# Hybrid decoder step: rooms for the first FFN weights, two tile scalings and the last output-projection units

## Chip, cores and metric

One Trainium2 chip, one core. The metric is the device time of one execution in microseconds. The kernel before runs in 2260.09 us (median of three runs, 2257.26 to 2260.82); the execution that the profiler recorded took 2260.48 us.

## What is computed

One layer of a hybrid decoder, for a prompt of 1024 tokens and a sample of 8 sequences with 8 tokens each. The part that matters here, from the reference:

```python
h = h + jnp.concatenate([o_gla, o_mla], axis=-1) @ lw['w_o']
y, conv_new = conv_ffn(rmsnorm(h, lw['g_ffn']), conv_prev, lw)
h = h + y
...
def conv_ffn(n, prev, lw):
    a = n @ lw['ffn_w_gate']
    c = n @ lw['ffn_w_up']
    ...
    y = (jax.nn.silu(conv) * c) @ lw['ffn_w_down']
```

`o_mla` of the sample comes from attention over a paged cache of 8192 past tokens for each of the 8 sequences; that is 64 blocks of 128 x 8 cached rows. `w_o` is 1024 x 1024, `ffn_w_gate` and `ffn_w_up` are 1024 x 2816.

## The kernel before, in words

All matrices are float32, held as a high and a low part (`split`, lines 115 to 117: ScalarE casts the high part, VectorE or GpSimd subtracts to get the low part), and a product is three matmuls (`mm3`, lines 139 to 141).

The work before the FFN is two interleaved programs. The *dense* one projects the prompt, runs its linear attention and its latent attention. The *cache stream* (`cache_stream`, L678) takes the 64 blocks of the sample's cache, n = 0 to 63. Block n passes through stages that overlap with those of its neighbours: `main` multiplies the pages with the absorbed weights (line 139 to 141, tile `ks`), ScalarE squares (L560), VectorE sums each two pages (L565, four such *slots* in a block); `stage_b` turns the sums into scaled scores (ACT L586 to L588, DVE L589 and L590, POOL L592 and L594, DVE L598 for the maxima, POOL L599), and splits the pages for the second product (ACT L603, POOL L604); `stage_c1` transposes the maxima on TensorE (tile `mt`, L616 and L625), subtracts and exponentiates (DVE L626, ACT L628 and L629, POOL L630); `stage_pv` multiplies with the pages (`cpv`, L645); `stage_c2` finishes a sequence after its last block (L667 to L676).

When the dense program has ended, 47 of the 64 blocks are done, and the output projection's *units* (`wo_units`, L1536) become the filler of the rest: a unit is one row tile t of 128 tokens, one half f of the 1024 columns, and a pair of the eight 128-row slices of `w_o`: six matmuls of 512 columns (L1432, L1435, L1436) and one addition into the residual on VectorE (L1439). There are four pairs, so 4 x 16 units; the generator's first step only loads. `place` (L574) is called at each slot and issues one unit from the seventh slot on, except at every eighth, until the counter is 49, that is until the first three pairs are through. The last pair's 16 units run through the tiles in the order 6, 7, 0, 3, 1, 4, 2, 5, both halves of a tile together. With a tile's second half its residual is complete and `normed` (L1587) follows: ScalarE squares and sums both halves (L1465), GpSimd makes the scale (L1466, L1467), ScalarE's queue stores the tile to DRAM (L1591), and `xnorm` (L1469) multiplies by the scale and the gain. `xnorm` has two forms, chosen by a bit mask `VIAP` over the tiles: one VectorE instruction (L1474), or a scaling on ScalarE (L1476) and a multiplication by the gain on GpSimd (L1477).

In the stream's *drain*, the last three steps with hardly any blocks left, the units are issued by hand. With "63rd" and "64th" for the blocks n = 62 and n = 63, the counts before are: 1 in `stage_c1` of the 63rd (and whatever is missing to 49), 3 in its `stage_pv`, 2 and 1 in `stage_c1` of the 64th, 5 in its `stage_pv`, 4 in its `stage_c2`.

Then come the FFN's operands. `turned_rest` transposes tiles 6 and 7 (L132, tile `xr`), `turned_pair` (L1657) transposes the pairs (0, 3), (1, 4), (2, 5) (L1663) and forms the sums of a Strassen-like scheme with seven products on blocks of 384 tokens: ScalarE's copies and casts (L1665, L116), VectorE's and GpSimd's sums and low parts (L1666 to L1672, L117). `down_sample` adds the sample's part (`ps_ds`, L1445, L1448), several rooms of SBUF are closed, `last_sums` splits the last two operands `t3` and `t4` (six casts on ScalarE, three subtractions each on GpSimd and VectorE), `normed(NT)` normalises the sample's 64 rows `hs`, and `ff_weights(0)` (L1699) loads and splits the first chunk of 128 FFN columns: four DMAs of 256 KB on SyncE's queue (L1705, tile `st`), eight operands in splits (`g0`, `g1`, `s2`, `s1`, `s4`, `s3`, `u1`, `u0`; casts of tile `wh`, low parts of tile `wl`), and between them four sums on GpSimd (L1712, L1713 for `s1` and `s2`; L1716, L1718 for `s4` and `s3`). `ff_chunk` (L1753) runs the seven products of tile `ps_gu` in the order g0, g1, s2, s1, s4, s3, u1, and the rest of the rows. There are 22 chunks.

The order of each engine's queue isn't the order of the text: the kernel is built with `schedule_with_timeline_sim=True`, and the framework sets each queue's order at build time by a model of the timeline, with the text's order as the priority. `behind()` (L570) and `keep_in_program_order` bind some TensorE work to its place.

Of the kernel before, what the change touches and what calls it, by code (L numbers as in the profile page):

```python
# [29 lines left out]
PLAN = ([0], [], [1, 2, 3])  # L30
VIAP = 20
GS0 = 1
# [13 lines left out]
def step_kernel(ctx: ExitStack, tc: tile.TileContext, A):  # L46
# [152 lines left out]
    z = {}  # L199
# [374 lines left out]
    def place():  # L574

        z["slot"] += 1
        if z["slot"] > 6 and z["slot"] % 8 and z["units"] < 49:
            fill(1)
# [27 lines left out]
    def stage_c1(o):  # L606
# [4 lines left out]
        drain = o.n - NB * 8 + 3  # L611
        if drain == 1:
            fill(49 - z["units"])
        elif drain == 2:
            fill(2)
        pe.transpose(mt[:, 0:P], o.ml.rearrange("p a c -> p (a c)"), ident)  # L616
# [21 lines left out]
    def stage_pv(o):  # L638
        nt, phl = o.nt, o.phl
        drain = o.n - NB * 8 + 3  # L640
        if drain > 0:
            fill(1 + 2 * drain)
        o.pv = pv = pm([P, 512], "cpv")
        for i in range(nt):
            pe.matmul(pv[:, 0:258], phl[:, i, :], o.ch[:, i, :], start=i == 0, stop=i == nt - 1)  # L645
        if (o.b, o.bi) == (NB - 1, 7):
            acc = z["late"][:, 0:258]
        else:
            acc = cp.tile([P, 258], F32, tag="pvs", name="pvs", bufs=2)
        if o.t is None:  # L650
            act.copy(acc, pv[:, 0:258])
        else:
            dve.scalar_tensor_tensor(acc, sums.pop(o.b), o.t, pv[:, 0:258], ALU.mult, ALU.add)
        sums[o.b] = acc

    def stage_c2(o):
# [15 lines left out]
        if b == NB - 1:  # L672
            fill(4)
        pt = pm([P, 512], "pt_ol")
# [919 lines left out]
    def fill(n):  # L1594
        for _ in range(n):
            z["units"] += next(z["fill"], done) is None
# [102 lines left out]
    def ff_weights(f):  # L1699
# [14 lines left out]
        w["s2"] = block(s2, dve)  # L1714
        w["s1"] = block(s1, dve)
        pool.tensor_tensor(g1, g1, s2, ALU.subtract)  # L1716
        w["s4"] = block(g1, dve)
# [35 lines left out]
    def ff_chunk(f):  # L1753
# [33 lines left out]
        if f + 1 < NF:  # L1787
            ff_weights(f + 1)
        conv(0, NP)
# [55 lines left out]
    rx2 = opened("xh2", side="right")  # L1845
    xb.update({nm: [z["xh2"].tile([P, 4, NP], F32R, name=f"x{nm}{s}") for s in "hl"] for nm in ("t4", "t3")})
    for t in range(3):
        last_sums(t)
    normed(NT)
    room["hp"].close()  # L1850
    fw, fv = opened("fw", side="right"), opened("fv", side="right")
    ff_weights(0)
    rt = opened("tp")
# [271 lines left out]
```

## Time and profile before

| | us |
|---|---|
| median of three runs | 2260.09 |
| profiled execution | 2260.48 |
| its span, first to last instruction | 2258.8 |
| around the span | 1.7 |
| TensorE busy | 2169.4 (96%) |
| VectorE busy | 1674.5 (74%) |
| ScalarE busy | 1338.8 (59%) |
| GpSimd busy | 1242.1 (55%) |

Times of rows are microseconds from the span's start. In a row of the timeline the columns are start, length, engine, line, operation, tile written and tiles read, shape, count; the bracket at the end is the engine's idle time just before the instruction and what ended it. Matmuls overlap: what a matmul costs TensorE is the distance from its start to the next one's. PEclk is the granted clock of TensorE as a share of its upper level.

### The profile page before, as it was taken

What the parts mean: (1) busy time and instruction counts of PE and PEld (TensorE: products, weight loads), DVE (VectorE), ACT (ScalarE), POOL (GpSimd) and SP (SyncE); (2) the same over time, 40 slices, a digit from 0 to 9 for tenths busy, and PEclk for the clock granted to TensorE, in tenths of its full rate; (3) what the DMA queues carried; (4) which work ended last, traced back from release to release, by engine and by line L of the source; (5) the groups of instructions that cost most, each with busy time, mean ns of one, the idle gap of its engine ahead of it and who ended that gap; (6) DMA issues with size and microseconds to landing.
All of it is one profiled execution on the core that took longest, in us unless ns stands there. A gap on an engine that the chain in (4) does not pass through costs nothing.

```text
span 2258.8 us, 38778 instructions
## 1 busy us (share of the span) xinstructions
PE 2169.4 (96%) x13591; PEld 1962.1 (87%) x13591; DVE 1674.5 (74%) x2608; ACT 1338.8 (59%) x3711; POOL 1242.1 (55%) x1332
## 2 busy tenths in 40 slices
PE   7999989999999999998999988999999999999999
PEld 6889978878888888887888877999999997888899
DVE  5775776467788888886878878888888876777642
ACT  5676766777778898886777765333333334222531
POOL 5675677567777777675454468656565640010200
PEclk9899999999999999999999988999999999999999
DMA  5343334413342222213322122332323224333131
GB/s 183 113 135 100 91 120 147 139 50 88 83 122 59 60 79 67 59 41 129 98 66 77 62 98 76 98 104 84 103 84 105 83 81 133 113 122 117 52 116 40
DMA packets 193461, 213.43 MB, mean 94 GB/s; under 512 B 41198, under 2 KB 145107, under 8 KB 193267
## 3 DMA queue, kind: packets, MB, share of 16 engines
q1 hardware_dynamic: 179603, 164.02, 23.5%
q0 software_dynamic: 12432, 42.48, 6.1%
q10 hardware_dynamic: 1232, 4.46, 0.5%
q8 instruction: 109, 1.79, 0.3%
q14 instruction: 85, 0.70, 0.1%
HBM read 168.34 MB, written 42.52 MB: 93 GB/s over the span
## 4 chain that ended last, share of the span: by engine, by line
PE 81%; DVE 7%; ACT 5%; DMA 3%; POOL 2%; issue 2%; SPq 0%; ACTq 0%; POOLq 0%; DVEq 0%
PE ps_gu L140 7%; PE ps_gu L141 7%; PE ps_gu L139 7%; PE ks L139 5%; PE ks L141 4%; PE ks L140 4%; PE ps_dn L139 4%; PE ps_dn L140 4%; PE ps_dn L141 4%; PE cpv L645 2%; PE ctp L522 2%; PE ps_lt L278 2%; PE ps_pj L139 2%; PE ps_pj L140 1%; PE ps_pj L141 1%
## 5 line engine op out<-in xcount | busy, mean ns | idle before, releaser
L560 ACT ACTIVATE csq<-ks 128x256 f32<-128x256 f32 x1040 | 392.5, 400 | 87.9 <-PE ks L141 79.2
L565 DVE TENSOR_REDUCE css<-csq 128x16 f32<-128x1024 f32 (+1 forms) x264 | 315.8, 1197 | 64.6 <-ACT csq L560 61.8
L116 ACT CAST wh<-st 128x512 fp32r<-128x512 f32 x176 | 108.4, 619 | 186.1 <-PE ps_gu L140 161.4
L139 PE MATMUL ks<-mv0h,cTh 128*128 128x320 f32 (+1 forms) x520 | 171.7, 332 | 6.6 <-ACT csq L560 2.9
L139 PE MATMUL ks<-mv1h,cTh 128*128 128x320 f32 (+1 forms) x520 | 170.6, 330 | 7.6 <-ACT sn L562 3.6
L604 POOL TENSOR_TENSOR chl<-craw,chl 128x1024 fp32r<-128x1024 f32 x64 | 141.3, 2208 | 57.6 <-ACT chl L603 57.0
L140 PE MATMUL ks<-mv1l,cTh 128*128 128x320 f32 (+1 forms) x520 | 154.0, 298 | 0.0
L140 PE MATMUL ks<-mv0l,cTh 128*128 128x320 f32 (+1 forms) x520 | 152.9, 296 | 0.0
L141 PE MATMUL ks<-mv0h,cTl 128*128 128x320 f32 (+1 forms) x520 | 148.5, 298 | 0.9 <-DVE cTl L117 0.8
L141 PE MATMUL ks<-mv1h,cTl 128*128 128x320 f32 (+1 forms) x520 | 148.8, 300 | 0.0
L630 POOL TENSOR_TENSOR phl<-sn,phl 128x512 fp32r<-128x512 f32 (+1 forms) x64 | 84.9, 1327 | 108.2 <-ACT phl L629 107.8
L1928 DVE TENSOR_TENSOR h<-h,ps_dn 128x512 f32<-128x512 f32 x160 | 107.7, 685 | 49.0 <-PE ps_dn L141 43.2
L117 DVE TENSOR_TENSOR wl<-st,wh 128x512 fp32r<-128x512 f32 x132 | 119.0, 903 | 29.6 <-ACT wh L116 29.6
L139 PE MATMUL ps_dn<-w,s 128*128 128x512 f32 x352 | 137.0, 393 | 2.3 <-ACT w L116 2.3
L140 PE MATMUL ps_dn<-w,s 128*128 128x512 f32 x352 | 137.6, 391 | 0.0
L141 PE MATMUL ps_dn<-w,s 128*128 128x512 f32 x352 | 136.9, 390 | 0.0
L1939 POOL TENSOR_TENSOR h<-h,raw 128x512 f32<-128x512 f32 x16 | 20.7, 1294 | 195.5 <-DMA raw<-dh 133.5
L117 POOL TENSOR_TENSOR wl<-st,wh 128x512 fp32r<-128x512 f32 x44 | 69.5, 1581 | 104.9 <-ACT wh L116 104.9
L117 DVE TENSOR_TENSOR cTl<-ctp,cTh 128x512 fp32r<-128x512 f32 (+1 forms) x136 | 90.1, 662 | 39.1 <-ACT cTh L116 38.1
L139 PEld LDWEIGHTS ks<-mv0h,cTh 128*128 128x128 f32 x520 | 98.9, 190 | 20.6 <-ACT sn L562 7.2
L139 PEld LDWEIGHTS ks<-mv1h,cTh 128*128 128x128 f32 x520 | 99.7, 192 | 19.4 <-ACT sn L562 7.0
L562 ACT COPY sn<-ks 128x64 f32<-128x64 f32 x520 | 116.4, 224 | 0.0
(662 smaller groups left out, 7974.3 us busy)
## 6 DMA issues: line engine op xcount, KB each, us to landing
stage<-w_in SPq DMA_DIRECT2D x48, 256.0 KB
st<-ffn_w_gate SPq DMA_DIRECT2D x44, 256.0 KB
st<-ffn_w_up SPq DMA_DIRECT2D x44, 256.0 KB
wr<-ffn_w_down SPq DMA_DIRECT2D x44, 256.0 KB
raw<-ds SPq DMA_DIRECT2D x44, 256.0 KB
raw<-ffn_w_down SPq DMA_DIRECT2D x44, 256.0 KB
ds<-cv SPq DMA_DIRECT2D x21, 512.0 KB
oraw<-doT SPq DMA_DIRECT2D x16, 256.0 KB
```

The lines of the kernel that those rows point to most:

```text
L116: act.copy(hi, src)
L117: (lo_eng or dve).tensor_tensor(lo, src, hi.bitcast(F32), ALU.subtract)
L139: pe.matmul(ps, ah, bh, start=first, stop=False)
L140: pe.matmul(ps, ah, bl, start=False, stop=False)
L141: return pe.matmul(ps, al, bh, start=False, stop=last)
L278: pe.matmul(ps, x, w, start=first, stop=last)
L560: act.activation(sq[:, f * 256:f * 256 + 256], ks[:, 0:256], AF.Square)
L562: act.copy(o.sn[:, g0 + i, :], ks[:, 256:320])
L565: dve.tensor_reduce(o.ss[:, g0 + i + 1 - n:g0 + i + 1, :].rearrange("p i h -> p (i h)"), sq2[:, :n].rearrange("p i (h n) -> p (i h) n", n= ...
L604: pool.tensor_tensor(ch[:, c0:c1, 128:256], src, ch[:, c0:c1, 0:128].bitcast(F32), ALU.subtract)
L630: pool.tensor_tensor(phl[:, :nt, 64:128], sb, phl[:, :nt, 0:64].bitcast(F32), ALU.subtract)
L1928: dve.tensor_tensor(h[:, t, cs], h[:, t, cs], ps, ALU.add)
```

## The change

Three things are changed. The mask `VIAP` becomes 192, tiles 6 and 7, where it was 20, tiles 2 and 4. `place` waits four slots after the counter has reached 49 and then issues one unit of the last pair at each slot, up to the counter 55, and the counts in the drain are changed: 1 and 1 in `stage_c1` of the 64th block, 3 in each `stage_pv`, all that is left in `stage_c2`. The room `fw` (the first four weight operands and the stages of the weights) is opened before `last_sums`, and `ff_weights` becomes a generator in two parts: the first part (loads, splits of `g0`, `g1`, `s2`, `s1` and the two sums that make `s1` and `s2`) stands before `last_sums` for the first chunk, the second part where it was.

```diff
-VIAP = 20
+VIAP = 192
...
         z["slot"] += 1
-        if z["slot"] > 6 and z["slot"] % 8 and z["units"] < 49:
+        if z["units"] < 49:
+            z["last"] = z["slot"] + 4
+            if z["slot"] > 6 and z["slot"] % 8:
+                fill(1)
+        elif z["slot"] > z["last"] and z["units"] < 55:
             fill(1)
...
         elif drain == 2:
-            fill(2)
+            fill(1)
...
         if drain > 0:
-            fill(1 + 2 * drain)
+            fill(3)
...
         if b == NB - 1:
-            fill(4)
+            fill(16)
...
         w["s1"] = block(s1, dve)
+        yield
         pool.tensor_tensor(g1, g1, s2, ALU.subtract)
...
-            ff_weights(f + 1)
+            for _ in ff_weights(f + 1):
+                pass
...
+    fw = opened("fw", side="right")
+    first = ff_weights(0)
+    next(first)
     for t in range(3):
         last_sums(t)
     normed(NT)
     room["hp"].close()
-    fw, fv = opened("fw", side="right"), opened("fv", side="right")
-    ff_weights(0)
+    fv = opened("fv", side="right")
+    for _ in first:
+        pass
```

## Rows read from the trace of the kernel before

**Rows 1.** The page's chain that ended last, shares of the span by engine.

```profile
PE 81%; DVE 7%; ACT 5%; DMA 3%; POOL 2%; issue 2%; SPq 0%; ACTq 0%; POOLq 0%; DVEq 0%
```

**Rows 2.** Stretches: length, busy by engine (instructions), PEclk, DMA share, GB/s.

```profile
1287.50:1312.00 24.50, 20.26 (x123) 17.50 (x121) 19.93 (x26) 17.82 (x59) 11.92 (x9) 0.93 0.13 44
1312.00:1340.30 28.30, 26.88 (x120) 21.54 (x120) 22.59 (x37) 16.86 (x42) 16.00 (x20) 0.94 0.31 121
1340.30:1362.40 22.10, 17.36 (x90) 13.03 (x89) 19.32 (x29) 16.93 (x33) 19.17 (x16) 0.77 0.29 96
1362.40:1368.30 5.90, 0.00 (x0) 0.00 (x0) 5.80 (x8) 5.65 (x13) 5.00 (x4) 0.85 0.20 44
1368.30:1390.90 22.60, 20.91 (x104) 18.89 (x104) 18.11 (x21) 11.45 (x21) 17.87 (x17) 0.89 0.27 83
1390.90:1875.00 484.10, 480.65 (x2896) 475.91 (x2896) 404.61 (x538) 182.38 (x360) 288.98 (x274) 1.00 0.29 93
```

**Rows 3.** Units' first matmuls (L1432), two stretches; L565's reductions on DVE.

```profile
1060.00:1287.50 227.50, 38.71 (x96) 18.37 (x96) 0.98 0.29 92
1287.50:1312.00 24.50, 0.79 (x2) 0.38 (x2) 0.93 0.13 44
...
1287.50:1312.00 24.50, 9.08 (x8) 0.93 0.13 44
```

**Rows 4.** Timeline of TensorE at the start of the drain.

```profile
1312.91 0.33 PE L616 MATMUL mt<-ident,ml 128*128 128x128 f32 x1 [1.87 <-POOL ml L599]
1313.75 0.43 PE L625 MATMUL mt<-ident,bm 64*128 64x64 f32 x2 [0.51 <-DVE mt L622]
...
1315.39 0.63 PE L1436 MATMUL ps_dn<-wdh,sl 128*128 128x512 f32 x1
...
1318.80 0.40 PE L1435 MATMUL ps_dn<-wdl,sh 128*128 128x512 f32 x1
1319.03 0.40 PE L1436 MATMUL ps_dn<-wdh,sl 128*128 128x512 f32 x1
```

**Rows 5.** Timeline: the scalings of tiles 6, 7 (DVE), 4 and 2 (ACT, POOL).

```profile
1321.60 1.28 DVE L1474 SCALAR_TENSOR_TENSOR h<-h,rs,gb 128x1024 f32<-128x1024 f32 x1
...
1324.62 2.34 DVE L1474 SCALAR_TENSOR_TENSOR h<-h,rs,gb 128x1024 f32<-128x1024 f32 x1
...
1340.45 1.15 ACT L1476 ACTIVATE h<-h,rs 128x1024 f32<-128x1024 f32 x1 [1.25 <-POOL rs L1467]
...
1341.68 2.35 POOL L1477 TENSOR_TENSOR h<-h,gb 128x1024 f32<-128x1024 f32 x1 [1.26 <-ACT h L1476]
...
1346.79 3.33 POOL L1477 TENSOR_TENSOR h<-h,gb 128x1024 f32<-128x1024 f32 x1 [0.22 <-ACT h L1476]
```

**Rows 6.** Timeline of ScalarE ahead of TensorE's first FFN product, and that product.

```profile
1363.23 0.63 ACT L1465 ACTIVATE junk<-hs 64x512 bf16<-64x512 f32 x1 [0.22 <-DVE hs L1456]
...
1363.86 0.60 ACT L116 CAST xt3h<-h 128x512 fp32r<-128x512 f32 x1
...
1367.66 1.12 ACT L116 CAST wh<-st 128x512 fp32r<-128x512 f32 x2
...
1368.31 0.69 PE L139 MATMUL ps_gu<-x11h,wh 128*128 128x384 f32 x1 [5.92 <-ACT wh L116]
```

**Rows 7.** Timeline of SyncE's queue: the last two loads of the first weights.

```profile
1344.74 0.92 SPq L1705 DMA_DIRECT2D st<-ffn_w_up  x2
```

**Rows 8.** Timeline of GpSimd, VectorE and TensorE in the first FFN chunk.

```profile
1364.54 4.63 POOL L117 TENSOR_TENSOR xt3l<-h,xt3h 128x512 fp32r<-128x512 f32 x3 [0.90 <-ACT xt3h L116]
...
1372.66 2.15 POOL L1713 TENSOR_TENSOR st<-st 128x512 f32<-128x512 f32 x1
...
1376.39 1.74 POOL L1718 TENSOR_TENSOR st<-st 128x512 f32<-128x512 f32 x1
...
1379.20 0.68 DVE L117 TENSOR_TENSOR wl<-st,wh 128x512 fp32r<-128x512 f32 x1
...
1380.67 0.33 PE L139 MATMUL ps_gu<-x22h,wh 128*128 128x384 f32 x1
```

## The prediction

> **What bounds the kernel now.** I began with the chain that ended last: 81% of the span lies on TensorE [rows 1]. So a change pays where TensorE stands still, or runs slowly, and nowhere else. The table of stretches says where that is [rows 2]. From 1390.9 us, soon after the start of the second FFN chunk, to 1875 us TensorE is busy 480.65 of 484.10 us: whatever comes earlier at 1390.9 ends earlier by as much. Ahead of it lie the five stretches that the change touches, 103.4 us long. TensorE is busy 85.4 us of them, so 18.0 us are idle: 4.2 at the stream's end, 1.4 in the drain, 4.7 while the operands are transposed, 5.9 in one piece before the first FFN product, 1.7 in the first chunk. Its clock is below its upper level in all five (0.77 to 0.94). The other engines tell what holds it. From 1340.3 to 1362.4 VectorE is busy 19.32 and GpSimd 19.17 of 22.10 us, so the transposes wait for the engines that empty their banks. In the 5.9 us piece nothing is missing but the first weights' high parts, which stand on ScalarE's queue behind other casts [rows 6].
>
> **Part 1, units in the stream.** How many units move follows from code and counts. By 1287.5 us the trace has 96 of the units' first matmuls, two to a unit: 48 units, so the counter is at 49, and the next ones come only with the drain, two matmuls up to 1312 us [rows 3]. Eight reductions follow 1287.5. The unit just done belongs to the first of them (with 17 blocks left there are 68 slots, and the 48th unit falls on slot 61: from slot 7 on, without 8, 16 and so on). `place` then waits for slots 62 to 65 and issues at 66, 67 and 68: three units, not the six that the limit of 55 would allow. The drain's counts then add up to 4, 7, 9, 12 and 16, against 1, 4, 7, 12 and 16 before; from the 64th block's `stage_pv` on, as many units have been issued as before. A unit is six starts of 0.23 us [rows 4], 1.4 us, so 4.2 us of matmuls go ahead of the drain. They lie where TensorE waits 1.87 us for the maxima of the 63rd block and 0.51 us for the next step [rows 4], and after that wait eight matmuls start 3.41 us apart in all (1315.39 to 1318.80) where the next distance is 0.23, eight of which are 1.84: 1.6 us lost to the lower level, 1.2 GHz, after an idle TensorE. Both gone: 2.4 + 1.6 = 4.0 us. Bounds: below, 0, if the three units only push the 64th block's `ks` matmuls, and with them its scores, by 4.2 us and the wait reopens later; above, 4.2, the whole of the moved work. I take 3.0, since both waits are for the 63rd block, which the moved units don't touch, but the 64th does start later. The additions on VectorE (three of some 0.7) fall where it is least loaded; the casts and loads of the last pair are called three slots sooner, on a SyncE queue with nothing urgent in it.
>
> **Part 2, scalings.** VectorE loses tiles 6 and 7, 1.28 + 2.34 us, and gains tiles 2 and 4 later, at 1.28 each if nothing disturbs, so its sum falls by about 1.1; ScalarE's two scalings of 1.15 and GpSimd's two products of 2.35 and 3.33 move from 1340 to 1350 us into the drain, where those engines are busy 16.9 and 16.0 of 28.3 us [rows 2, 5]. The way to tile 2's operands shortens from 1.15 + 3.33 to about 1.3 us, and GpSimd goes from the last scaling into the operands with no pause, so up to 3.2 us could come out of the transposes. Against it, VectorE, itself full there, gets 2.56 us more in that stretch, and in the drain GpSimd's scalings may stand ahead of the last block's scores. Between -3.2 and +4.7 (both products at 2.35 uncovered on the chain) I take 0, because the two late effects have about the same size and opposite sign. Clashes have a price here: the same VectorE instruction takes 1.28 us at one time and 2.34 at another, and GpSimd's 2.35 or 3.33 [rows 5], so about 1 us per meeting. The Trainium skill (SBUF — State Buffer, section "Who interferes with whom") puts it more harshly: a VectorE instruction with two SBUF inputs and a GpSimd instruction that reads SBUF exclude each other, and the later one waits for the whole of the other. By that rule the two moved products could hold VectorE for all of their length in the drain, and the sum below would end at -1.8 instead of -6.5 (the third rival). The rows show waits of 1 us, and I go by them.
>
> **Part 3, first weights.** The four loads are issued by 1345.7 us, as soon as the stages are free [rows 7], 18 us before any use; opening the room sooner moves no load. What it moves is the priority. Now the two casts of `g0` and `g1` start at 1367.66, behind six casts of `t3` and `t4` that begin at 1363.86, and TensorE starts 0.65 us after them, having waited 5.92 us [rows 6]. With the weights' casts first, they take 1363.86, and the product starts 3.8 us earlier, near 1364.5. Upper bound: the whole 5.9 us, plus 2.5 us of clock (0.89 over 22.6 us, so some 5 us at half speed), 8.4; lower: 0, see the first rival. What becomes late: `t3` and `t4` by four casts, some 2.3 us, and by GpSimd's two sums, 3.9 us by L1713 and, for the other, L1718. GpSimd's `t3` subtractions end at 1369.2 now, and the `t4` product they and VectorE feed comes after 1380.67, when the product ahead of them starts: over 10 us of cover [rows 8]. GpSimd is the next limit. It runs from 1346.79 to 1378.1 with few pauses, and the sums of `s4` and `s3` keep their place at the end of it. Now `s4`'s low part is ready at 1379.9, 0.8 us ahead of its product [rows 8]; a TensorE that is over 6 us early will wait there for one or two. I take 3.5 for the part, since the four products before that one are what it can run through first.
>
> **The sum.** 3.0 + 0 + 3.5 = 6.5 us off the profiled execution's 2260.48 (span 2258.8 and 1.7 around it), which stands 0.4 above the median: 2254.0 us, 0.27% below the median.
>
> **Rivals.** *GpSimd's queue decides.* Reordering doesn't shorten GpSimd's list, and it is busy 17.87 of 22.60 us in the first chunk and 5.00 of 5.90 before. If `s4` and `s3` come only as much earlier as GpSimd's pauses allow, 0.90 us ahead of `t3` [rows 8] and about as much again among the 2.9 us of the transposes' stretch [rows 2], TensorE starts early and waits later: 1.8 and little from part 1, about 2258. For it: the near margin at 1380.67. Against: part 1 brings GpSimd's list forward too. 15%. *The queues don't move.* Each queue's order is set by a model at build time; the weights' casts or the three units may land where they were: 2260, 7%. *VectorE is held in the drain.* If each moved product keeps VectorE's additions off for its whole 2.35 us, and these stand on the chain there, 4.7 us come back: 2260.5 - 6.5 + 4.7 = 2258.7. For it: tile 7's scaling took 1.06 us longer than tile 6's [rows 5]. Against: VectorE has 5.7 us free in the drain [rows 2]. 6%. It is what the Trainium skill's rule above would do here. *The drain stalls, and the kernel is slower.* If the scalings of tiles 6 and 7 stand on GpSimd's queue ahead of the last block's L592, L594 or L630, TensorE waits for the scores once its units are used up. Two products at 3.33 are 6.7 us, and 1.6 more at the lower clock; with part 1's gain gone and part 3's 3.5 kept that gives 2260.5 + 8.3 - 3.5 = 2265. It decides once the hold-up exceeds what the units between cover: there are five between the 64th block's maxima and its `stage_pv`, 7 us, less what the chain itself needs. For it: GpSimd's maxima already set the 1.87 us wait. Against: the queue has 12 us free in the drain. 10%.
>
> **How the numbers follow.** My forecast has the remaining 62%. The range reaches down to the sum with parts 1 and 2 near their best and part 3 between its value and its bound, 4.0 + 2.0 + 6.0 = 12 off, 2248.5, and up to no gain at all, 2260.5, which takes in the first three rivals; the slower rival and larger gains are left out. Two tenths of a per cent, 4.5 us, is about what a measurement of this kernel can tell from no change. Faster by more needs 2255.6 or less, which the forecast holds: 0.62. Within it lie the first three rivals: 0.28. Slower: 0.10.
>
> **What would show it.** Right: three units among the stream's last slots, 1305 to 1313 us, and no wait of over 1 us at the 63rd block's maxima; the first `ps_gu` matmul at 1361 us or earlier (3 from part 1, 3.8 from part 3); casts of `wh` ahead of those of `t3`; TensorE's idle time from 1287 to the second chunk down from 18 to about 12 us. Wrong: a first `ps_gu` product that comes early and a pause before that of `s4` or `s3` that takes it back; a pause at `mt` or `cpv` in the drain released by GpSimd; or a first product still behind six casts.

## The result: slower by 4 us, and the profile after

The changed kernel takes 2264.16 us (median of 22 runs, 2256.13 to 2270.58) against 2259.16 us for the kernel before, measured beside it on the same chips (22 runs): a ratio of 1.0019 [1.0011, 1.0028], so 4.3 us slower. Measured twice more, once under another name with the same order of instructions on every engine (e13 and e14 below), it gave 1.0011 [1.0002, 1.0019] and 1.0017 [1.0007, 1.0027]. The cost is thus some 2.5 to 4.3 us, where 6.5 us of gain were forecast. The profiled execution after took 2262.32 us, its span 2260.6.

The same six stretches as in [rows 2], each moved to the same event of the code, the end of the last so that its length is that of before (view: stretches; length, busy time by engine with instructions, PEclk, DMA share, GB/s):

```profile
1287.10:1311.60 24.50, 21.49 (x133) 19.24 (x132) 19.86 (x26) 18.44 (x62) 11.46 (x11) 0.93 0.19 65
1311.60:1338.30 26.70, 23.42 (x112) 18.39 (x111) 19.82 (x31) 17.41 (x42) 20.61 (x20) 1.00 0.27 101
1338.30:1363.80 25.50, 19.47 (x90) 15.07 (x88) 22.56 (x35) 15.40 (x33) 15.42 (x13) 0.67 0.29 91
1363.80:1369.80 6.00, 0.14 (x2) 0.01 (x1) 5.36 (x7) 5.60 (x13) 3.71 (x3) 0.94 0.20 44
1369.80:1392.50 22.70, 20.73 (x104) 19.43 (x105) 19.60 (x21) 11.55 (x21) 18.17 (x17) 0.87 0.27 82
1392.50:1876.60 484.10, 480.61 (x2897) 475.83 (x2896) 402.29 (x539) 182.71 (x360) 286.27 (x274) 1.00 0.29 93
```

Four lines matter. The second stretch, the drain, is 1.6 us shorter and its granted clock is up from 0.94 to 1.00. The third, the transposes, is 3.4 us longer, VectorE is busy 22.56 us of it (before 19.32) and the clock is down from 0.77 to 0.67: that takes the gain and more. The fourth, TensorE's pause before the first FFN product, is 6.00 us as against 5.90: part 3 did nothing. The last is the same to 0.3 us: from the rest rows' first product to the first down product, 484.46 us before and 484.20 after.

TensorE's timeline in the drain after, which answers to [rows 4]:

```profile
1303.83 0.40 PE L1437 MATMUL ps_dn<-wdh,sh 128*128 128x512 f32 x1
...
1306.86 0.40 PE L1437 MATMUL ps_dn<-wdh,sh 128*128 128x512 f32 x1
...
1310.80 0.39 PE L1437 MATMUL ps_dn<-wdh,sh 128*128 128x512 f32 x1
...
1313.59 0.27 PE L621 MATMUL mt<-ident,ml 128*128 128x128 f32 x1
1314.86 0.43 PE L630 MATMUL mt<-ident,bm 64*128 64x64 f32 x2 [1.00 <-DVE mt L627]
...
1321.16 1.23 PE L650 MATMUL cpv<-chl,phl 128*128 128x258 f32 x8 [0.60 <-POOL phl L635]
...
1325.45 0.33 PE L621 MATMUL mt<-ident,ml 128*128 128x128 f32 x1 [1.68 <-POOL ml L604]
```

Three units stand among the stream's last slots, and the maxima of the 63rd block (1313.59) no longer wait. But waits have reopened behind them: 1.00 us at the 63rd block's next step, 0.60 us at its `cpv` product, and at the 64th block's maxima 1.68 us, released by GpSimd's L604. Why GpSimd is late there, the timelines of ScalarE and GpSimd after tell:

```profile
1309.43 0.36 ACTq L1596 DMA_DIRECT2D dh<-h  x1
...
1314.09 1.15 ACT L1481 ACTIVATE h<-h,rs 128x1024 f32<-128x1024 f32 x1 [2.12 <-DMA dh<-h]
1315.14 0.33 ACT L591 ACTIVATE cy<-css,epst 128x64 f32<-128x64 f32 x1
...
1315.32 2.40 POOL L1482 TENSOR_TENSOR h<-h,gb 128x1024 f32<-128x1024 f32 x1 [1.45 <-ACT h L1481]
...
1318.78 1.08 POOL L597 TENSOR_TENSOR sn<-sn,cy 128x512 f32<-128x512 f32 x1
...
1322.30 2.40 POOL L1482 TENSOR_TENSOR h<-h,gb 128x1024 f32<-128x1024 f32 x1
...
1325.16 0.24 POOL L604 COPY ml<-ml 128x64 f32<-128x64 f32 x1
```

`xnorm` scales a tile in place, and `normed` stores the same tile to DRAM first. Tile 6's store is issued at 1309.43 and ScalarE, which now scales this tile, waits 2.12 us for it, until 1314.09. Behind that on its queue stands L591, the first step of the last block's scores; and the two products on GpSimd stand ahead of L597 and L604, the steps that lead to the last block's maxima. None of the prediction's sentences speaks of the store.

ScalarE ahead of the first FFN product, and that product, as in [rows 6]:

```profile
1365.41 0.60 ACT L116 CAST xt3h<-h 128x512 fp32r<-128x512 f32 x1
...
1369.14 1.12 ACT L116 CAST wh<-st 128x512 fp32r<-128x512 f32 x2
...
1369.80 0.69 PE L139 MATMUL ps_gu<-x11h,wh 128*128 128x384 f32 x1 [5.87 <-ACT wh L116]
```

The order is that of before: six casts of `t3` and `t4`, the squares, and only then the weights. Moving the code moved nothing on the queue.

To set runs side by side, the table gives times from the 62nd block's maxima (L616 before, L621 after; read from the timelines), since what lies ahead differs by some us from execution to execution of the same code. The last unit ends 0.23 us, the distance from one matmul to the next, after its last matmul starts; the bank's column is the start of ScalarE's first copy (L1665 before).

| kernel | 64th block's maxima | last unit ends | first transposed bank copied | first FFN product | end of span |
|---|---|---|---|---|---|
| before | 21.15 | 39.04 | 46.47 | 67.15 | 957.64 |
| e3 (queues of before) | 20.92 | 38.81 | 46.46 | 68.66 | 959.81 |
| after | 24.67 | 37.52 | 46.79 | 69.02 | 959.82 |
| e13 (after again) | 25.00 | 37.85 | 46.22 | 68.09 | 962.52 |
| e14 (queues of after) | 24.79 | 37.65 | 46.92 | 69.14 | 960.12 |
| e1 | 23.79 | 39.19 | 44.49 | 67.38 | 958.00 |
| e2 | 19.36 | 37.35 | 48.15 | 69.49 | 961.00 |
| e12 | 24.60 | 37.46 | 46.72 | 68.93 | 959.61 |
| e16 (e12 again) | 23.24 | 36.10 | 43.57 | 65.96 | 956.55 |
| e9 | 23.18 | 36.03 | 44.01 | 65.88 | 956.67 |
| e15 | 23.86 | 40.35 | 48.00 | 71.37 | 962.19 |
| e18 | 21.06 | 39.15 | 47.86 | 72.37 | 963.17 |

Executions with the same queues differ: before and e3 by 1.5 us at the first FFN product, after, e13 and e14 by 2.7 us at the end, e12 and e16 by 3.0 us at both. So a row names the place of a cost, and the medians its size.

### The profile page after: what moved, and what is told of

It is laid out like the page before. It is cut to its first block, busy times and chain, and to the rows that moved or that the text cites. A ratio compares the mean times of both kernels' runs of the same rounds, so it can differ in the third digit from the quotient of the medians.

```text
span 2260.6 us, 38768 instructions
## 1 busy us (share of the span) xinstructions
PE 2168.8 (96%) x13591; PEld 1962.0 (87%) x13591; DVE 1671.3 (74%) x2608; ACT 1337.9 (59%) x3711; POOL 1237.5 (55%) x1332
## 4 chain that ended last, share of the span: by engine, by line
PE 79%; DVE 8%; ACT 5%; DMA 4%; POOL 3%; issue 2%; SPq 0%; DVEq 0%; POOLq 0%; ACTq 0%
PE ps_gu L141 7%; PE ps_gu L140 7%; PE ps_gu L139 7%; PE ks L139 5%; PE ks L141 4%; PE ks L140 4%; PE ps_dn L140 4%; PE ps_dn L141 4%; PE ps_dn L139 3%; PE cpv L650 2%; PE ctp L522 2%; PE ps_pj L139 2%; PE ps_lt L278 2%; PE ps_pj L140 2%; PE ps_pj L141 2%
## 5 line engine op out<-in xcount | busy, mean ns | idle before, releaser
L565 DVE TENSOR_REDUCE css<-csq 128x16 f32<-128x1024 f32 (+1 forms) x264 | 315.7, 1197 | 64.9 <-ACT csq L560 62.1
L609 POOL TENSOR_TENSOR chl<-craw,chl 128x1024 fp32r<-128x1024 f32 x64 | 141.3, 2208 | 56.9 <-ACT chl L608 56.3
L635 POOL TENSOR_TENSOR phl<-sn,phl 128x512 fp32r<-128x512 f32 (+1 forms) x64 | 84.8, 1325 | 105.0 <-ACT phl L634 104.6
```

The costliest lines, as they stand in the source:

```text
L565: dve.tensor_reduce(o.ss[:, g0 + i + 1 - n:g0 + i + 1, :].rearrange("p i h -> p (i h)"), sq2[:, :n].rearrange("p i (h n) -> p (i h) n", n= ...
L609: pool.tensor_tensor(ch[:, c0:c1, 128:256], src, ch[:, c0:c1, 0:128].bitcast(F32), ALU.subtract)
L635: pool.tensor_tensor(phl[:, :nt, 64:128], sb, phl[:, :nt, 0:64].bitcast(F32), ALU.subtract)
```

## The experiments

**e1 to e4: the parts alone.** e1 is the first part alone, e2 the mask alone, e3 the third part alone, e4 the changed kernel with no tile on ScalarE and GpSimd.

```
e1:  the hunks of place() and of the four fill() calls only
e2:  -VIAP = 20     +VIAP = 192     (nothing else)
e3:  the hunks of ff_weights, ff_chunk and the opening of fw and fv only
e4:  (on after)  -VIAP = 192    +VIAP = 0
```

> The kernel before with part 1 alone (units in the stream, new counts in the drain), mask still 20. Theory A (the mask costs the time: the scaling in place of tiles 6 and 7 has to wait for their store to DRAM on ScalarE's queue, and GpSimd's two products stand ahead of the last block's scores): no wait on the store in ScalarE's queue, the 64th block's maxima reach TensorE by 1322 us, the units end by 1337 us, the first ps_gu matmul starts at 1366.5 us or earlier, time 2 us or more below the kernel before. Rival B (the moved units delay the last block and the gain is lost again in VectorE's queue, whatever the mask): units end early but the first ps_gu matmul is at 1368 to 1370 us, time within 2 us of the kernel before or above it.

> The kernel before with the mask 192 alone. Theory A: ScalarE waits 2 us or more for tile 6's store, the 64th block's maxima come 2 us or more later than 1322.3 us, the first ps_gu matmul at 1370 us or later, time 2 us or more above the kernel before. Rival B: the mask alone is harmless, first ps_gu matmul within 1 us of 1368.3 us, time within 2 us.

> The kernel before with part 3 alone (room opened sooner, weights' first part called sooner). After's trace shows the casts of the weights still behind those of t3 and t4, so both theories expect no change: the same order on every queue, first ps_gu matmul within 0.5 us of 1368.3 us, time within 2 us of the kernel before. A gain of 3 us or more would say that the part works and the other two cost more than they seem to.

> The kernel after with the mask 0: all eight tiles scaled by VectorE. Theory A: no wait for a store on ScalarE's queue, GpSimd free of products in the drain, the 64th block's maxima by 1322 us; VectorE has 2 scalings more than in the kernel before (2.6 us) in a stretch where it is nearly full, so the first ps_gu matmul within 1367 to 1369.5 us, below after's 1369.8 us, time between the kernel before and 3 us below after. Rival B: as after, first ps_gu matmul 1369.5 to 1371 us, time like after's.

Measured against 2259.22 us for before (33 runs): e1 2260.55 us, 1.0001 [0.9992, 1.0010]; e2 2261.60 us, 1.0008 [0.9999, 1.0017]; e3 2259.13 us, 0.9997 [0.9985, 1.0008]; e4 2263.93 us, 1.0016 [1.0007, 1.0025]. Part 3 is empty: e3 has the order of before on all five engines. Part 1 is worth nothing by itself, which falls on its lower bound; theory A expected 2 us or more. In e1 the wait at the 63rd block's maxima is gone, but three others have opened. TensorE's waits of e1 in the drain, then the two instructions behind the second of them:

```profile
1315.18 1.06 PE L132 MATMUL pt<-ident,h 128*128 128x128 f32 x8 [1.28 <-DVE h L1478]
1322.14 1.23 PE L649 MATMUL cpv<-chl,phl 128*128 128x258 f32 x8 [1.15 <-POOL phl L634]
1333.32 1.24 PE L649 MATMUL cpv<-chl,phl 128*128 128x258 f32 x8 [2.30 <-POOL phl L634]
...
1319.67 1.29 DVE L1478 SCALAR_TENSOR_TENSOR h<-h,rs,gb 128x1024 f32<-128x1024 f32 x1 [0.75 <-ACT junk L1469]
...
1319.75 2.34 POOL L634 TENSOR_TENSOR phl<-sn,phl 128x512 fp32r<-128x512 f32 x1
```

They sum to 4.7 us, against 2.4 us in [rows 4]. The last pair shows the price of a meeting: GpSimd's L634 takes 1.28 us when nothing is beside it (in after, as L635, at 1319.83) and here 2.34 us, because it begins 0.08 us behind a scaling of 1.29 us on VectorE and starts its own work when that ends.

The mask alone moves the cost where the prediction had a gain: in e2 the units end 1.7 us sooner and the first bank is copied 1.7 us later. Between the two, the stretch from the last unit to the first copy (columns as above), before first, then e2:

```profile
1340.20:1347.63 7.43, 5.79 (x44) 4.49 (x44) 6.74 (x10) 6.12 (x13) 5.59 (x7) 0.90 0.84 283
```

```profile
1332.95:1343.75 10.80, 7.24 (x44) 5.88 (x43) 9.84 (x16) 5.20 (x14) 3.81 (x4) 0.71 0.66 214
```

VectorE is full, 9.84 of 10.80 us, and GpSimd busy only 3.81 us; before, VectorE was busy 6.74 and GpSimd 5.59 of 7.43 us.

Theory A's own sign is missing in e2: it expected a wait of 2 us or more for tile 6's store and the 64th block's maxima 2 us later, and they come 1.8 us sooner (19.36 us, before 21.15). ScalarE of e2, the first step of the last block's scores and the scaling of tile 6:

```profile
1306.18 0.35 ACT L586 ACTIVATE cy<-css,epst 128x64 f32<-128x64 f32 x1 [1.29 <-DVE css L565]
...
1315.27 1.15 ACT L1476 ACTIVATE h<-h,rs 128x1024 f32<-128x1024 f32 x1 [0.50 <-DMA dh<-h]
```

Here the scaling stands behind the scores and waits 0.50 us. Only with part 1, which completes tile 6 sooner, does it land ahead of them. e4, with no product on GpSimd at all, is as slow as after: so the loss isn't GpSimd's products in the drain alone. Its last scaling, on VectorE right before the transposes (1349.04), waits 1.96 us for a store too.

**e5 and e6: part 3 made to do what it says.** The last operands' splits and the last rows' norm are bound behind the second cast of the weights (e5 without part 1, e6 with it, both with the mask of before). `casts` collects the casts in the order of the calls; the lines that fill it aren't shown.

```
...
     next(first)
-    for t in range(3):
-        last_sums(t)
-    normed(NT)
+    with tc.issue_after(casts[1].ins):
+        for t in range(3):
+            last_sums(t)
+        normed(NT)
```

> The kernel before with part 3 and a bond that puts last_sums and the sample's normalisation behind the weights' second cast on ScalarE's queue, so that part 3 happens. Theory A (part 3 as written moves nothing, the order it means is worth most of its 3.8 us): the time from the last ps_ds matmul's end to the first ps_gu matmul falls from 5.7 to 6.1 us to 2.5 us or less, and 2.5 us or more of it are left at the first matmul of the rest rows (89.8 us after the 62nd block's maxima in the kernel before); time 2 to 4 us below the kernel before. Rival C (GpSimd's queue decides): the first ps_gu matmul comes 3 to 4 us earlier, the rest rows' first matmul less than 1.5 us earlier, time within 1.5 us of the kernel before.

> Parts 1 and 3 with the same bond, mask 20. Theory A: as e5, and with part 1, which alone gave nothing, nothing is added: time 2 to 4 us below the kernel before. Rival C: within 1.5 us of it. If part 1's 2 us at the end of the drain had been eaten by the late weights, both together would give 5 us or more.

Measured against 2256.91 us (23 runs): e5 2261.14 us, 1.0017 [1.0007, 1.0027]; e6 2263.55 us, 1.0027 [1.0015, 1.0038]. The bond works: the weights' casts come first, and TensorE's first FFN product starts 62.13 us after the anchor (the 62nd block's maxima), 5.0 us earlier than before. TensorE of e5, the first product with its successor's wait, and all of its waits from 1358 to 1410 us:

```profile
1360.26 0.44 PE L140 MATMUL ps_gu<-x11h,wh 128*128 128x384 f32 x1 [1.19 <-ACT wh L116]
...
1363.20 0.69 PE L142 MATMUL ps_gu<-x11h,wl 128*128 128x384 f32 x1 [1.79 <-DVE wl L117]
```

```profile
PE ps_gu L140 <- ACT wh L116: 2.8, 2, 1.6
PE ps_gu L142 <- DVE wl L117: 2.5, 2, 1.8
PE ps_gu L140 <- DVE cv L1827: 1.9, 1, 1.9
PE ps_gu L140 <- DVE q L1803: 0.5, 1, 0.5
PE ps_gu L140 <- ACT xrh L116: 0.3, 1, 0.3
```

The waits (total, times, longest) sum to 8.0 us, and all are for high or low parts or for VectorE's work on the first two chunks. Behind the high parts stands GpSimd, whose sum ScalarE's next cast waits for:

```profile
1369.38 1.14 ACT L116 CAST wh<-st 128x512 fp32r<-128x512 f32 x2 [4.11 <-POOL st L1716]
```

VectorE is busy for the whole 20 us of 1375 to 1385 and 1400 to 1410. Times from the anchor tell where the 5.0 us go. The `t4` product of the first chunk comes 2.2 us earlier than before (81.49 against 83.66 us), the `t2` product of the second 2.8 us (100.27 against 103.09), its `t4` product 0.4 us (111.99 against 112.35), and so does the first down product: 4.7 us are given back, about half in the first chunk and half in the second. (The rest rows' first product, 5.1 us earlier, misleads: twelve matmuls that stood ahead of it stand behind it in e5.) So in this trace part 3, made to work, gains almost nothing. Why both medians are above before's, when e5's one trace ends no later, isn't settled by these runs.

**e7 and e8: four tiles on ScalarE and GpSimd** (2, 4, 6 and 7), with and without parts 1 and 3, to take the late scalings off VectorE.

```
e7: (on after)  -VIAP = 192  +VIAP = 212        e8: (on before)  -VIAP = 20  +VIAP = 212
```

> The kernel after with the mask 212: tiles 6 and 7 as after, tiles 2 and 4 as before, all four by ScalarE and GpSimd. Theory D (the late scalings of tiles 2 and 4 on VectorE cost the time): from the units' end to the first ps_gu matmul 28 to 30 us as in the kernel before (after: 31.5), time within 1.5 us of the kernel before or below it. Rival E (the early scalings of tiles 6 and 7 on ScalarE and GpSimd cost it, by the wait for the store and by GpSimd's products ahead of the 64th block's scores): time like after's, 3 us or more above the kernel before.

> The kernel before with the mask 212 and nothing else. Theory D: VectorE has 3.6 us less to do than in the kernel before and nothing more later, so 0 to 3 us below the kernel before. Rival E: 1 to 3 us above it, as the mask 192 alone was.

Measured: e7 2264.38 us, 1.0030 [1.0018, 1.0042]; e8 2263.83 us, 1.0028 [1.0018, 1.0038]. VectorE is relieved (6.15 of 6.82 us between the units and the first copy, which comes 2.2 us sooner than in after), and the kernel is slower still. The relieved VectorE of e7 stands and waits:

```profile
1349.78 1.69 DVE L1479 SCALAR_TENSOR_TENSOR h<-h,rs,gb 128x1024 f32<-128x1024 f32 x1 [2.35 <-DMA dh<-h]
```

That is tile 5's scaling, the last before the transposes, 5.1 us after its store was issued on ScalarE's queue (1344.66). In e8 the same wait is 3.16 us. So the late scalings on VectorE are not the whole cost either, and the store has become a suspect.

**e9, e10, e11: no scaling waits for a store.** The store sends the gain's rows in place of the tile's, so the last residual adds those and the layer's output is lost: the three are probes of the time alone. `row_scale` returns its last square for the bond.

```
-        row_scale(t)
+        with tc.issue_after(row_scale(t)):
+            act.dma_start(dh[t], z["gb"][:P if t < NT else R])
         x = hrows(t)
-        act.dma_start(dh[t], x)
```

> The changed kernel, but what each tile's store to DRAM sends is the gain's rows in place of the tile's (same size, same queue, each bound behind its tile's squares), so no scaling in place waits for a store to land; the last residual then adds the gain's rows in place of h. Theory F (what the change costs is ScalarE's wait of 2.12 us for tile 6's store, which pushes the 64th block's maxima and all behind them): no wait on dh in the drain, the 64th block's maxima within 22.5 us of the 62nd's instead of 24.7, and a ratio to before of 1.0000 to 1.0008 in place of 1.0019. Rival G (GpSimd's products of tiles 6 and 7 ahead of the last scores, and VectorE's list at the end of the units, are the cost; the store wait is covered): ratio 1.0015 to 1.0025 as without it, the maxima still 24 us or more after.

> Before with four tiles (2, 4, 6, 7) scaled by ScalarE and GpSimd, and the gain's rows stored in place of h's as in the run of that kind on the changed kernel. With the real stores this mask gave 1.0028, and VectorE waited 3.16 us for a tile's store right before the transposes. F: without that wait the transposes' stretch (end of the units to the first FFN product, 34.0 us with the stores) falls to 30 us or less and the ratio to 1.0000 to 1.0008. Rival G: GpSimd's two extra products are the cost, the stretch stays at 32 us or more, ratio 1.0020 to 1.0030.

> Before with the gain's rows stored in place of h's, bound as in the two others: the control. Before's trace has no wait on these stores over 0.1 us, so F and G both expect 0.9995 to 1.0005. If it is faster by more than 0.001, the stores have a price in every version, and the two others are to be read against this one.

Measured against 2259.30 us (34 runs): e9 2258.75 us, 1.0001 [0.9991, 1.0011]; e10 2264.96 us, 1.0022 [1.0011, 1.0033]; the control, e11, 2266.85 us, 1.0029 [1.0019, 1.0039]. e9 goes theory F's way: its maxima come at 23.18 us (22.5 was expected, after has 24.67), its first FFN product 3.1 us sooner than after's, and the ratio is that of before. But the control was to be neutral and is 6.6 us slower: built with this edit, its queues come in another order. In e11 a scaling on VectorE beside a product on GpSimd takes 3.46 us instead of 1.28, right ahead of the transposes. The queues of e9 differ from after's too (on GpSimd L597 and L599, steps of the last block's scores, stand one place further ahead). So e9 goes F's way without proving it, and e10 says nothing about it.

**e12: the store as early as it can be.** Nothing is left out.

```
+        x = hrows(t)
+        sp.dma_start(dh[t], x)
         row_scale(t)
-        x = hrows(t)
-        act.dma_start(dh[t], x)
```

> The changed kernel with each tile's store issued from SyncE's queue ahead of the tile's squares, the data unchanged. F: stores start about 1 to 1.5 us earlier, ScalarE's wait for tile 6's store falls from 2.1 to about 1 us, and the ratio from 1.0019 to about 1.0010. G: no change, 1.0015 to 1.0025.

Measured: 2259.10 us, 1.0001 [0.9991, 1.0011]. The ratio fell below the 1.0010 expected, and yet the trace shows the wait of 2.07 us and the stages of after. The expectation of an earlier store was wrong: on either queue it starts when the last addition to the tile ends, 8.5 and 8.65 us after the anchor. The order of the queues isn't that of after either: on GpSimd L597 and L599 stand one place further ahead, as in e9. In this execution that made no difference: all its columns in the table lie within 0.25 us of after's.

**e13 to e16: one chip for the changed kernel, its twin, a third way to take the wait away, and e12 again.** e13 is after unchanged; e14 is parts 1 and 2 alone; e16 is e12. e15 calls tile 6's scaling behind the last block's activations:

```
-        act.activation(a[:, :nt], y[:, :nt], AF.Square)
+        sq = act.activation(a[:, :nt], y[:, :nt], AF.Square)
...
+        if o.n == NB * 8 - 1:
+            if 'post' in z:
+                with tc.issue_after(sq.ins):
+                    z.pop('post')()
...
-        xnorm(t, x, pool if VIAP >> t & 1 else dve)
+        if t == 6:
+            z["post"] = lambda: xnorm(t, x, pool)
+        else:
+            xnorm(t, x, pool if VIAP >> t & 1 else dve)
```

> The changed kernel itself, on the chip and against the runs of before that the next three share. Theory F (the changed drain costs: ScalarE waits 2.12 us for tile 6's store ahead of the 64th block's scores) expects a ratio of 1.0010 to 1.0025, as at first (1.0019). Rival H (the earlier ratio was partly luck: the run with the early store has the same trace and 1.0001) expects 1.0000 to 1.0010.

> Before with the first two parts alone (units in the stream, mask 192); every engine's order of instructions is that of the changed kernel, so any difference to the run above is what a measurement can't tell. F and H both expect the same as the run above within 0.001.

> The changed kernel with tile 6's scaling put behind the 64th block's three activations (Ln, Exp, Square) on ScalarE's queue, where its store has long landed; nothing is left out. F: no wait on dh on ScalarE, GpSimd's first product stands behind the 64th block's scores, its maxima come 21 to 22.5 us after the 62nd block's (24.67 in the changed kernel), and the ratio is 0.0015 or more below that of the changed kernel in this call. Rival G (GpSimd's products and VectorE's list are the cost wherever the store lands): the maxima come earlier, but the first FFN product stays at 68.5 us or more from the 62nd block's maxima, and the ratio stays within 0.001 of the changed kernel's.

> Once more the changed kernel with each store issued from SyncE's queue ahead of the squares. Its first trace has the same wait (2.07 us) and the same stages as the changed kernel's, since the store starts when the last addition ends on either queue. F and H: within 0.001 of the changed kernel's ratio in this call. If it is 0.0015 or more below it, as the first two measurements of the two would have it, something that the stages do not show sets them apart.

Measured against 2258.63 us (35 runs): e13 2261.65 us, 1.0011 [1.0002, 1.0019]; e14 2263.18 us, 1.0017 [1.0007, 1.0027]; e15 2263.72 us, 1.0021 [1.0012, 1.0029]; e16 2259.06 us, 0.9997 [0.9987, 1.0007]. The version with the early store is without the loss a second time, and e12 and e16, two executions of one kernel, show a part of how. ScalarE's scaling of tile 6 and TensorE's `cpv` behind it, on the timelines of e12:

```profile
1311.64 1.15 ACT L1481 ACTIVATE h<-h,rs 128x1024 f32<-128x1024 f32 x1 [2.07 <-DMA dh<-h]
...
1319.93 1.23 PE L650 MATMUL cpv<-chl,phl 128*128 128x258 f32 x8 [1.75 <-POOL phl L635]
```

and of e16:

```profile
1311.35 1.16 ACT L1481 ACTIVATE h<-h,rs 128x1024 f32<-128x1024 f32 x1 [0.71 <-DMA dh<-h]
...
1319.64 1.23 PE L650 MATMUL cpv<-chl,phl 128*128 128x258 f32 x8 [0.41 <-POOL phl L635]
```

The stretch from the last unit to the first copied bank (columns as above), e12 first, then e16:

```profile
1335.85:1345.11 9.26, 7.07 (x44) 5.89 (x43) 9.01 (x14) 4.33 (x13) 3.39 (x4) 0.69 0.66 211
```

```profile
1335.55:1343.02 7.47, 5.00 (x43) 3.70 (x42) 7.42 (x13) 4.29 (x13) 3.39 (x4) 1.00 0.56 192
```

The wait for the store is 1.36 us shorter in e16, the one at `cpv` 1.34 us, and the 64th block's maxima and the units' end come 1.36 us sooner. In the next stretch TensorE has its upper level, 2.4 GHz, throughout in e16, and 0.69 in e12; there the difference grows, to 2.97 us at the first FFN product and 3.06 us at the end. These are two executions, but of one program, and all else in the drain is equal. So 1.36 us are the wait's. Whether the other 1.7, which come with the clock, are its doing too isn't shown: ahead of the copies TensorE stands still for 1.87 us in e12 and 1.88 in e16, and in that stretch the clock falls in e12 alone.

Set beside the other traces of parts 1 and 2, the 64th block's maxima go with the wait in three different orders of the queues: 24.60 to 25.00 us where it is 2.07 to 2.45 us (e12, after, e14, e13), 23.24 and 23.18 us where it is 0.71 (e16) or none (e9).

Why the wait differs, the DMA packets tell. The store is 128 packets of 4 KB, and closes with 16 of 4 B; of these, 15 have ended 2.3 us after the issue in e12 and in e16. Packets' starts from 2.28 us after the issue on, in 40 slices of 0.043 us (view: DMA, its line of GB/s; 95 is a packet of 4 KB, 381 one of 16 KB of the kind "instruction"), e12 first:

```profile
GB/s 0 0 95 0 0 0 0 381 0 0 0 0 0 0 0 0 0 0 0 0 0 0 0 0 0 0 0 0 95 0 0 0 0 0 0 0 0 0 0 0
```

```profile
GB/s 0 95 0 0 0 0 0 95 0 0 0 381 0 0 0 0 0 0 0 0 0 0 0 0 0 0 0 0 0 0 0 0 0 0 0 0 0 0 0 0
```

In e12 the instruction packet (2.60 to 3.53 us after the issue) comes ahead of the store's last 4 KB, and the sixteenth closing packet ends at 3.97 us; in e16 it comes just behind them, and the store closes at 2.76 us. Tile 6's store in before, with no such packet beside it, closes at 2.29 us; in after, e13 and e14, with one, at 4.09, 4.43 and 4.07. So the long wait goes with a load of instructions beside the store, which then closes 1.7 to 2.1 us later. That the two share a DMA engine fits these times; the record doesn't name the engine.

e15 took the wait away for certain (nothing waits for `dh` in the drain), and is no faster than after: rival G's numbers, 71.37 us and a ratio within 0.001 of e13's. The scaling of tile 7 on GpSimd now begins together with one on VectorE; their timelines with what follows, of e15:

```profile
1324.95 3.49 DVE L1483 SCALAR_TENSOR_TENSOR h<-h,rs,gb 128x1024 f32<-128x1024 f32 x1
1328.96 0.35 DVE L631 TENSOR_SCALAR_CACHE_REDUCE mt<-mt,bm 128x128 f32<-128x128 f32 x1
...
1324.95 2.40 POOL L1486 TENSOR_TENSOR h<-h,gb 128x1024 f32<-128x1024 f32 x1
1327.30 3.17 POOL L609 TENSOR_TENSOR chl<-craw,chl 128x1024 fp32r<-128x1024 f32 x1
...
1329.42 0.43 PE L634 MATMUL mt<-ident,bm 64*128 64x64 f32 x2 [2.09 <-DVE mt L631]
```

VectorE's 1.28 us become 3.49, which is GpSimd's 2.40 and 1.1 of its own; then GpSimd's L609, 2.19 us alone, takes 3.17 behind VectorE. The last block's new maximum (L631) stands behind the scaling on VectorE's queue, TensorE waits 2.09 us for it, and the units end 2.8 us later than in after. The wait for a store has been replaced by a wait for another engine.

**e17 and e18: the early store elsewhere.** e17 is the changed kernel with mask 20 and the early store, e18 is before with the early store.

> The changed kernel with tiles 2 and 4 on ScalarE and GpSimd as before (so part 1 is what is left of the change) and each store issued from SyncE's queue ahead of its tile's squares. F (what costs is a scaling that waits for its store ahead of the last scores, and this kernel scales tiles 6 and 7 on VectorE, late enough): as part 1 alone, 0.9990 to 1.0005, units' end 38.5 to 39.3 us after the 62nd block's maxima. Rival K (the early store is worth 3 us by itself, whichever tiles are scaled where): 0.9980 to 0.9990.

> Before with each store issued from SyncE's queue ahead of its tile's squares, nothing else. F: no scaling waits for a store in before, so nothing changes, 0.9995 to 1.0007. K: 0.9980 to 0.9990.

Measured against 2258.71 us (12 runs): e17 2268.36 us, 1.0037 [1.0024, 1.0051]; e18 2267.04 us, 1.0037 [1.0022, 1.0051]. Neither theory expected that; K is excluded, and F's "nothing changes" too. In e17 two scalings on VectorE wait 0.56 and 0.82 us for a store and then take 3.09 and 3.16 us instead of 1.28, and TensorE waits 2.56 us for a new maximum behind the first of them. In e18, VectorE's last scaling and, from SyncE's queue, the two last stores:

```profile
1351.68 1.28 DVE L1474 SCALAR_TENSOR_TENSOR h<-h,rs,gb 128x1024 f32<-128x1024 f32 x1 [1.57 <-DMA dh<-h]
...
1342.71 4.15 SPq L1590 DMA_DIRECT2D dh<-h  x2
```

Tile 5, the last before the transposes, now waits 1.57 us for its store, and the first FFN product comes 5.2 us later than before. The wait is 1.57 of the 5.2 us; the queues' order has changed as well, and what the rest comes from isn't settled. No version that was run beats the kernel before.

## Why the prediction was wrong

**Part 3, 3.5 us: the step that failed first.** "With the weights' casts first, they take 1363.86" took the order of the code for the order of the queue. It was the case of the second rival (7%), that the queues don't move: e3 has every engine's order of before, after has six casts ahead of the weights, and the first product waits 5.87 us where it waited 5.92. The first rival, that GpSimd's queue decides in the first chunk, is what e5 showed once the order was forced: ScalarE's cast waits 4.11 us for GpSimd's sum, VectorE's work takes the rest in the second chunk, and 4.7 of 5.0 us are given back. With that a premise fell too: "whatever comes earlier at 1390.9 ends earlier by as much" didn't hold for the second chunk, since VectorE was full there. The upper bound of 8.4 and the value of 3.5 had no ground; 0, the lower bound, was right.

**Part 1, 3.0 us: the moves were right, the gain was not.** Three units, not six; at slots 66 to 68; no wait left at the 63rd block's maxima: all as worked out. Alone (e1) the units end when they did before, 39.19 us after the anchor; the 1.0 to 1.5 us that they end sooner in after come with the mask, which takes scalings off VectorE there (e2: 1.7 us). The lower bound named the reason, "the wait reopens later", and the text then took 3.0 because the waits were for the 63rd block. They reopened at `cpv` and at the 64th block.

**Part 2, 0 us: the loss was missed.** It lies within the part's bounds (-3.2 to +4.7), but not for the reasons given. Two steps failed. First, the list of what moves, scalings and products, left out that the tile is scaled in place behind its own store: 4.7 us from issue to the scaling's start in after, 5.1 in e7. As long as the scaling came late on VectorE (before) nothing waited for it; on ScalarE, ahead of L591, the last block's scores wait. It takes parts 1 and 2 together: in e2 the scaling came behind the scores. The versions with the early or the replaced store (e9, e12, e16: 0.9997 to 1.0001) are about 3 us faster than after (1.0011 to 1.0019). That this is the wait is likely and not shown: their queues are in another order, e12's one trace has the wait in full, and e15, which removed it for certain, moved another queue. Shown is 1.36 us of it, between e12 and e16, and the wait reached 2 us only where a load of instructions lay beside the store. Second, "the way to tile 2's operands shortens" forgot that VectorE's two late scalings lie ahead of the transposes: in e2 the stretch from the last unit to the first copied bank grew from 7.43 to 10.80 us with VectorE full. e7 shows that taking them back to GpSimd, with four tiles there, is worse. The division of before, tiles 2 and 4, has the lowest time of those run: 192 gives 1.0008 (with an interval that reaches 1), none (with part 1) 1.0016, four tiles 1.0028.

**The meetings of VectorE and GpSimd** were priced at "about 1 us", and the stricter rule of the Trainium skill (SBUF — State Buffer, section "Who interferes with whom": the two exclude each other, and the one that comes second waits until the first has ended) was set aside because "The rows show waits of 1 us". That was a wrong reading of [rows 5], and the trace of before agrees with the rule. The two instructions that were met there:

```profile
1323.67 2.21 POOL L604 TENSOR_TENSOR chl<-craw,chl 128x1024 fp32r<-128x1024 f32 x1
...
1346.61 1.29 DVE L1474 SCALAR_TENSOR_TENSOR h<-h,rs,gb 128x1024 f32<-128x1024 f32 x1 [0.69 <-POOL rs L1467]
```

Tile 7's scaling of 2.34 us began at 1324.62 while GpSimd was at work on L604 from 1323.67 for 2.21 us, so it waited until 1325.88 and had 1.08 us of its own behind that; GpSimd's 3.33 us, from 1346.79, are 1.11 us of waiting for a VectorE scaling that ended at 1347.90, and 2.22 of its own. A wait of 1 us there is what was left of the other instruction. With both starting together it is all of it: 3.49 us in e15, and 3.46 in e11, where VectorE's record even begins 0.04 us ahead of GpSimd's.

**The rivals.** The one that ended on the other side had the right place and nearly the right number. It said that TensorE would wait if "the scalings of tiles 6 and 7 stand on GpSimd's queue ahead of the last block's L592, L594 or L630", at 2265 us; after has tile 6's product ahead of L597 (L592 before), tile 7's ahead of L604, and a wait of 1.68 us at the 64th block's maxima, and it took 2264.16. Its price of 8.3 us was too high and its 3.5 us for part 3 were not there; the two errors nearly cancel, so the closeness of the number is luck. It had 10% because GpSimd has 12 us free in the drain. Free time on an engine says nothing of where the instruction stands: ScalarE's wait for the store made GpSimd's product start at 1315.32 and not before. What the prediction's last part called wrong, "a pause at `mt` or `cpv` in the drain released by GpSimd" and "a first product still behind six casts", are both in the trace.

## What to carry to other kernels

Before an instruction is moved to another engine, list what it overwrites and who still reads that: a store that nobody waited for becomes a wait as soon as the in-place update comes early, and it holds whatever stands behind the update on the new engine's queue. Moving lines of code is not moving work where a model orders the queues: look at the order that was built before pricing the move. And where a VectorE scaling met a GpSimd instruction here, the second waited for what was left of the first, up to all of it (3.49 us in e15): the price of a meeting goes by the length of the instruction that is met, not by an average of what rows show.

## What the runs showed of the hardware that was not expected

A 512 KB store of a tile to DRAM kept the tile for 4.7 us (after, e12), 5.1 us (e7) and 5.0 us (e8) from its issue to the start of the instruction that waits for it, and for 3.4 us in e16, an execution of e12's kernel. The store alone closes 2.3 us after its issue (before, tile 6); where it was long, a 16 KB packet of instructions lay beside it, and the last of its 16 closing packets came at 4.0 to 4.4 us. With the same queues (after, e13, e14), the 62nd block's maxima, 1300 us into the kernel and ahead of everything that the change touches, came at 1300.78, 1297.28 and 1297.68 us. The time goes with TensorE's mean granted clock: a line through the 33 runs of before beside e1 to e4, and one through the 23 beside e5 to e8, falls by 1.2 us for each 0.001 of it (their means: 2259.6 us at 0.9835, 2257.4 us at 0.9843); the other three groups of runs of before give 1.0 to 1.5 us. A change of a few us can only be told from that with many runs on one chip, and two kernels with identical queues still gave 1.0011 and 1.0017.
